# Stacking the query latent's 64-row remainder into one 128-row operand in a two-layer encoder trunk

## The chip, the cores and the metric

The kernel runs on one core of a Trainium2 chip. The metric is the device time of one execution in microseconds; three runs of the kernel before gave 1157.86 to 1158.56 us, median 1158.54 us.

## The reference

Two layers work on 256 rows of width 2048, all in float32: a gated spatial mixer (layer 0) and a latent attention (layer 1). Each is wrapped in RMS norms and shift, scale and gate that come from a condition vector. The change touches only the query path of layer 1:

```python
cq, ckv, k_rope, z = jnp.split(h @ w_in, [o1, o2, o3], axis=-1)       # o1 = 448
q = (rms_norm(cq, q_norm_g) @ w_uq).reshape(B, S, MLA_HEADS, QK_NOPE_DIM + QK_ROPE_DIM)   # 16 heads, 128 + 64
kv = (rms_norm(ckv, kv_norm_g) @ w_ukv).reshape(B, S, MLA_HEADS, QK_NOPE_DIM + V_HEAD_DIM)
q_nope, q_rope = q[..., :QK_NOPE_DIM], q[..., QK_NOPE_DIM:]
...
q_rope = apply_rope(q_rope, cos[:, None, :], sin[:, None, :])
o = chunk_causal_attention(q_nope, q_rope, k_nope, k_rope, v)
y = o.reshape(B, S, MLA_WIDTH) * jax.nn.silu(z)
return y @ w_out
```

The query's latent is 448 wide, so its product with `w_uq` contracts over 448 = 3 x 128 + 64.

## The kernel before, in words

Every large product is taken in three float32r products that stand for one float32 product. Each operand is split into a high part (a rounding cast on ScalarE) and a low part (what is left, a subtraction on VectorE); TensorE adds up high x high, high x low and low x high in PSUM. `mm` (line 184, its matmul on line 185) issues each of them.

Weights come through the class `Stream`. `weights` (line 92) makes an item: a load on SyncE's queue into one of six raw buffers, and a stage that splits it into `h` and `l` (lines 71 and 72), each out of seven buffers. `get` hands the next split item to a product and lets the stages run some items ahead. The order of loads and stages is the order in which items are listed; the engines take their instructions in the order in which the program is written (the schedule is manual), and each waits only for what it reads or for a buffer to come free.

In layer 1 the latents are computed first (chunks `pm_0`, `pm_1`), normalised per block of 128 rows in `norm_latent` (line 1014, ScalarE writes `qn` and `kvn`), then turned in `turn_latent` (line 1033) so that the latent's width lies on partitions: four transposes on TensorE for two chunks, a scaled copy on ScalarE for the high part, a subtraction on VectorE for the low part. Chunk 3 of the query latent is only 64 wide and fills 64 partitions (`ws`). The per-column gains come from `rows_b`, a tile filled by small loads on GpSimd's queue at the start (lines 200 to 207) and turned by TensorE in `turn_rows`.

Then come eight pairs of heads. `q_unit` (line 1116) makes the queries of four heads and runs four times, for `q4` = 0 to 3; `kv_unit`, `scores`, `turn_p`, `weigh` and `turn_o` run once for each pair, with products of other weights (`fill`) between them. One `q_unit` has

- `qr`: the rope part, for two row blocks, each a group of products summed into one half of a PSUM bank (64 columns of each of four heads, 256 columns),
- `rope` (line 1002), four VectorE operations for each block that read that bank and write `qr` to SBUF,
- `qn`: the part without rope, two banks of two heads, each head a group of products with 256 columns, copied out and split by ScalarE (`qH`, line 190) and VectorE (`qL`, line 191),
- later, after the `k` products of `kv_unit`, the transposes `qrT`.

That is six groups in one `q_unit` and 24 in all. A group has four chunks of the latent with three products each:

```python
for k in range(4):
    (h, l), (xh, xl) = ws[k], xs[k]
    mm(o, h[:, cs], xh, k == 0, False)
    mm(o, h[:, cs], xl, False, False)
    mm(o, l[:, cs], xh, False, k == 3)
```

For `k` = 3 the operands have 64 rows. The product banks (`acc_bank`, pool `pm`) are four. In the second, third and fourth `q_unit` two of them hold a half-done fill product, and the program makes the first product of the second `qn` bank wait for the last `rope` operation that reads the `qr` bank (line 1009 for block 1).

Of the kernel before, what the change touches and what calls it, by code (L numbers as in the profile page):

```python
# [26 lines left out]
KVR = 512  # L27
NEG = -1e30
# chunks of adaLN's rows: (first, number, the first projection's visit before which they come)
STEPS = ((0, 2, 0), (2, 2, 24), (4, 2, 45), (6, 2, 78), (8, 4, 115), (12, 4, 162))  # L30
# how far the splitting of weights runs ahead of their products, and where other work lies between them
# [19 lines left out]
# from layer 0 to layer 1: T, F, H, L turn, modulate and split block b's quarter q; g, b are products of block 0 and  # L51
# of block 1, s splits weights, c and e are what is left of layer 0
PLAN = "e1 e1 e1 e1 T00 T01 s1 F00 F01 H00 L00 H01 e1 e1 L01 T02 T03 g1 c1 F02 H02 c1 g1 g1 L02 s1 c1 c1 g1 c1 F03 c1 g1 H03 g1 L03 T11 s1 T10 F11 F10 H10 L10 g1 s1 b1 H11 b1 L11 T12 F12 H12 L12 s1 T13 b1 F13 H13 b1 b1 b1 L13 b1"
# buffers on chip
# [5 lines left out]
class Stream:  # L60
    """Weights on their way to TensorE: each item is loaded, then split into the two float32r parts, some steps
    before the products that take it. Other work that keeps step with the loads lies between the items."""
# [29 lines left out]
    def weights(self, name, src, rows=P, slot=None):  # L92
        """src: gk * rows rows, gn columns"""
        gk, gn = src.shape[0] // rows, src.shape[1]
        box = self.raw_item(name, gk, gn, [(lambda r: r[0:rows], src.rearrange("(k p) n -> p k n", p=rows))])

        def stage():
            raw = box["raw"][0:rows]
            if slot:
                h = [slot(f"{name}h_{j}", (P, gn), F32R) for j in range(gk)]  # L100
                l = [slot(f"{name}l_{j}", (P, gn), F32R) for j in range(gk)]
                for j in range(gk):
                    self.split(raw[:, j, :], h[j], l[j])
                self.ready.append((h, l))
                return
            h = self.wp.tile([P, gk, gn], F32R, tag="wh", name=name + "h", bufs=SPLIT_BUFS)
            l = self.wp.tile([P, gk, gn], F32R, tag="wl", name=name + "l", bufs=SPLIT_BUFS)
            self.split(raw, h[0:rows], l[0:rows])
            self.ready.append((h, l))

        self.stages.append((len(self.loads), True, stage))
# [23 lines left out]
def spread(main, extra):  # L135
    """the items of extra evenly between those of main"""
    if not main:
        return
    done = 0
    for i, m in enumerate(main):  # L140
        m()
        want = -(-len(extra) * (i + 1) // len(main))
        while done < want:
            extra[done]()
            done += 1
# [3 lines left out]
def tile_trunk(  # L149
# [56 lines left out]
    nc.gpsimd.dma_start(out=rows_b[35:36, 0:QR - 384], in_=mla_q_norm_g[:, 384:QR])  # L206
# [63 lines left out]
    def ada_items(name, src, width, state):  # L270
        """src(k0, nk): the columns of nk row chunks, [P, nk, width] or with a pair of column ranges between"""
        nk = 1024 // width
        todo = []
        for k in range(KD):
            def add(k=k):
                if k % nk == 0:
                    state["box"] = ST.raw_item(
                        f"{name}_{k}", nk, width,
                        [(lambda r, v=v: (r if v is None else r.rearrange("p k (t n) -> p k t n", t=2)[:, :, v, :]), a)
                         for v, a in src(k, nk)])  # L280

                def stage(box=state["box"]):
                    if k == 0:
                        state["acc"] = sp.tile([P, 1024], F32, tag="acc", name=f"acc_{name}", bufs=2)[:, 0:width]
                    acc, raw, w = state["acc"], box["raw"][:, k % nk, :], sc[:, k:k + 1]
                    if k == 0:
                        nc.vector.tensor_scalar_mul(acc, raw, w)
                    else:
                        nc.vector.scalar_tensor_tensor(acc, raw, w, acc, op0=ALU.mult, op1=ALU.add)  # L289

                ST.hook(stage)
            todo.append(add)
        return todo
# [11 lines left out]
    def ada_put(l, k, n, ps_shift, ps_scale):  # L305
        """shift and scale of chunks k .. k + n from the sums"""
# [15 lines left out]
    def ada_range(l, k0, nk):  # L322
        """shift and scale of nk column chunks"""
        st = {}
        n = nk * P
        return ada_items(
            f"ada_{l}_{k0}",
            lambda k, m: [(t, ada_rows(l, k, m, t * D + k0 * P, n)) for t in range(2)],
            2 * n, st) + [lambda: ST.hook(ada_cols(l, k0, nk, st))]

    def ada_gate(l):
        """gate times post_g, as columns"""
# [20 lines left out]
    def spread_gate(l):  # L353
        """the gate as rows on all partitions, by way of a row in DRAM"""
# [36 lines left out]
    def chain(*fns):  # L391
        """the first now, each of the others one step later"""
        fns[0]()
        if len(fns) > 1:
            deferred.append(lambda: chain(*fns[1:]))

    def chunk_tasks(name, ks, lhs, evac, per=2):
        """one 512-column chunk of a product: tasks for both blocks, one pair for each granule of the weights"""
# [26 lines left out]
    # normalised, modulated rows turned for TensorE  # L425
# [24 lines left out]
    def hT_steps(k0, nk):  # L450
        """the same in steps that lie apart, each engine's part on its own"""
# [36 lines left out]
    # the first projection's cells: row chunks of h taken as their shift and scale come  # L488
# [42 lines left out]
    # the first two chunks' shift and scale, on the way to the first product: TensorE takes a part of the rows itself  # L531
# [18 lines left out]
    def first_split():  # L550
        """the first weights' parts row chunk by row chunk, each as the products need it"""
# [70 lines left out]
    def uq_items(q4):  # L622
        c0, cw = q4 * 4 * QK, 4 * QK
        return [lambda k=k: ST.weights(f"uq_{q4}_{k}", mla_w_uq[k * P:min(k * P + P, QR), c0:c0 + cw],
                                       min(P, QR - k * P)) for k in range(4)]
# [8 lines left out]
    def fills(z, a, b):  # L634
        """what lies between the steps of a pair of heads, and what is left for after the last"""
# [332 lines left out]
    def go(n):  # L968
        """the next n granules' products of block 0"""
# [44 lines left out]
    def norm_latent(b):  # L1014
# [4 lines left out]
        nc.scalar.mul(t[:, 0:QR], l0[:, 0:QR], rq)  # L1019
        qn.append(t)  # L1020
# [12 lines left out]
    def turn_latent(src, width, gcol, name, k, H, L):  # L1033
# [5 lines left out]
        ws = [(i, min(P, width - (k + i) * P)) for i in range(2)]  # L1039

        def turn():
            for i, w in ws:
                for b in range(NB):
                    nc.tensor.transpose(out=ps[0:w, i * 256 + b * P:i * 256 + (b + 1) * P],
                                        in_=src[b][:, (k + i) * P:(k + i) * P + w], identity=ident)

        def high():
            for i, w in ws:
                nc.scalar.mul(h[0:w, i, :], ps[0:w, i * 256:(i + 1) * 256], gcol(k + i)[0:w, :])

        def low():
            for i, w in ws:
                nc.vector.scalar_tensor_tensor(l[0:w, i, :], ps[0:w, i * 256:(i + 1) * 256], gcol(k + i)[0:w, :],
                                               h[0:w, i, :].bitcast(F32), op0=ALU.mult, op1=ALU.subtract)
# [3 lines left out]
    # shared rope keys, once above zeros and once below, for the heads of a pair  # L1058
# [31 lines left out]
    turn_latent(qn, QR, qg_col, "cq", 0, cqH, cqL)  # L1090
    run(t[1:2])
    turn_latent(qn, QR, qg_col, "cq", 2, cqH, cqL)
    run(t[2:3])
    turn_latent(kvn, KVR, kvg_col, "ck", 0, ckH, ckL)
    run(t[3:4])
    turn_latent(kvn, KVR, kvg_col, "ck", 2, ckH, ckL)
# [19 lines left out]
    def q_unit(q4):  # L1116
        gs = take(4)
        ws = [(h[0:min(P, QR - k * P), 0, :], l[0:min(P, QR - k * P), 0, :]) for k, (h, l) in enumerate(gs)]
        xs = []
        for k in range(4):  # L1120
            w = min(P, QR - k * P)
            xs.append((cqH[k // 2][0:w, k % 2, :], cqL[k // 2][0:w, k % 2, :]))
        ps = acc_bank(f"qr_{q4}")
        for b in range(NB):
            bs = slice(b * P, (b + 1) * P)
            o = ps[:, b * 256:(b + 1) * 256]
            for k in range(4):
                (h, l), (xh, xl) = ws[k], xs[k]
                hr = h.rearrange("p (h r) -> p h r", r=QK)[:, :, NOPE:QK]
                lr = l.rearrange("p (h r) -> p h r", r=QK)[:, :, NOPE:QK]  # L1130
                mm(o, xh[:, bs], hr, k == 0, False)
                mm(o, xh[:, bs], lr, False, False)
                mm(o, xl[:, bs], hr, False, k == 3)
# [5 lines left out]
        for p in range(2):  # L1139
            ps = acc_bank(f"qn_{q4}_{p}")  # L1140
            for i in range(2):
                o = ps[:, i * 256:(i + 1) * 256]
                cs = slice((2 * p + i) * QK, (2 * p + i) * QK + NOPE)
                for k in range(4):
                    (h, l), (xh, xl) = ws[k], xs[k]
                    mm(o, h[:, cs], xh, k == 0, False)
                    mm(o, h[:, cs], xl, False, False)
                    mm(o, l[:, cs], xh, False, k == 3)
# [247 lines left out]
```

## Time and profile before

| | |
|---|---|
| median of three runs | 1158.54 us (1157.86 to 1158.56) |
| profiled execution | span 1157.2 us from the first to the last instruction; the page gives no other time for it |
| TensorE busy | 98% of the span, 5705 matmuls |
| VectorE, ScalarE, GpSimd busy | 77%, 49%, 2% |
| DMA | 303.57 MB, mean 262 GB/s |
| mean granted TensorE clock | 0.998 |

The page gives shares over the whole span; the attention stage that the change touches lies from about 897 to 1075 us. A timeline row has the start, the duration, the engine, the line, the operation and, in brackets, how long the engine stood idle before it and for whom. A matmul's duration includes its passage through the array, so matmuls overlap: their pace is the distance between two starts.

### The profile page before, as it was taken

The page shows a single profiled execution, that of the slowest core. Times are in us where ns is not written, and L with a number is a line of the kernel's source. Part 1 is how long each engine was busy: PE and PEld are TensorE (multiplying, and loading weights), DVE is VectorE, ACT ScalarE, POOL GpSimd, SP SyncE. Part 2 cuts the span into 40 slices and gives each one's busy share as a digit, 9 for nine tenths or more (in the row PEclk, how much of TensorE's full clock was granted, in tenths as well). Part 3 has the DMA queues.
Part 4 walks back from the last instruction along what each step waited for, and adds up shares of the span by engine and source line. Part 5 has one row for each costly group of instructions (what it writes and reads, how often), then busy time and mean ns, then how long its engine had stood idle before and what let it go on. Part 6 is the DMA issues. An engine that isn't in the chain of part 4 may idle for free.

```text
span 1157.2 us, 15835 instructions
## 1 busy us (share of the span) xinstructions
PE 1132.1 (98%) x5705; PEld 958.9 (83%) x5705; DVE 892.2 (77%) x1187; ACT 566.8 (49%) x811; POOL 20.4 (2%) x46
## 2 busy tenths in 40 slices
PE   5999999999999999999999999999999999999997
PEld 5788878888888888888888888888888989999885
DVE  4889898978987887888787878668777557558655
ACT  3764334354546655545443444456554445445541
POOL 1000000000000000000001000000000000000000
PEclk9999999999999999999999999999999999999999
DMA  9999898978887886888689999954988245245672
GB/s 317 328 322 321 273 364 290 370 254 277 298 293 232 288 272 230 280 272 284 226 315 371 356 318 373 360 175 148 342 310 293 61 136 166 68 145 183 226 271 86
DMA packets 157855, 303.57 MB, mean 262 GB/s; under 512 B 11961, under 2 KB 28960, under 8 KB 157776
## 3 DMA queue, kind: packets, MB, share of 16 engines
q1 hardware_dynamic: 155808, 297.05, 75.0%
q0 software_dynamic: 1936, 5.49, 1.7%
q8 instruction: 45, 0.74, 0.3%
q14 instruction: 34, 0.28, 0.1%
q10 hardware_dynamic: 32, 0.01, 0.0%
HBM read 300.39 MB, written 2.11 MB: 261 GB/s over the span
## 4 chain that ended last, share of the span: by engine, by line
PE 87%; DMA 4%; DVE 4%; ACT 2%; issue 2%; SPq 0%; DVEq 0%; ACTq 0%
PE pi L185 23%; PE piz L185 15%; PE po L185 15%; PE pm L185 11%; PE pp L185 8%; PE qn L185 3%; DMA wi<-in_sgu_w_in_dram 2%; PE k L185 2%; PE v L185 2%; PE s L185 2%; PE o L185 1%; PE qr L185 1%; PE pada L301 1%; PE mix L185 1%; DMA first<-in_ada_w_dram 1%
## 5 line engine op out<-in xcount | busy, mean ns | idle before, releaser
L289 DVE SCALAR_TENSOR_TENSOR acc_ada<-ada,sc,acc_ada 128x1024 f32<-128x1024 f32 (+1 forms) x135 | 148.6, 1100 | 1.1 <-DMA ada<-in_ada_w_dram 0.2
L289 DVE SCALAR_TENSOR_TENSOR acc_gate<-gate,sc,acc_gate 128x1024 f32<-128x1024 f32 x60 | 76.6, 1277 | 0.6 <-DMA gate<-in_ada_w_dram 0.6
L669 DVE TENSOR_TENSOR part<-pi,part 128x512 f32<-128x512 f32 x92 | 59.6, 682 | 4.8 <-PE pi L185 4.7
L71 ACT CAST wi_6h<-wi 128x1024 fp32r<-128x1024 f32 x24 | 25.1, 1051 | 42.3 <-DMA wi<-in_sgu_w_in_dram 35.8
L71 ACT CAST wi_8h<-wi 128x1024 fp32r<-128x1024 f32 x24 | 25.2, 1050 | 27.8 <-DMA wi<-in_sgu_w_in_dram 18.2
L71 ACT CAST wi_4h<-wi 128x1024 fp32r<-128x1024 f32 x24 | 25.2, 1050 | 27.5 <-DMA wi<-in_sgu_w_in_dram 24.3
L72 DVE TENSOR_TENSOR wi_10l<-wi,wi_10h 128x1024 fp32r<-128x1024 f32 x24 | 29.3, 1219 | 6.8 <-ACT wi_10h L71 6.8
L72 DVE TENSOR_TENSOR wi_12l<-wi,wi_12h 128x1024 fp32r<-128x1024 f32 x24 | 29.2, 1217 | 5.2 <-ACT wi_12h L71 5.2
L72 DVE TENSOR_TENSOR wi_6l<-wi,wi_6h 128x1024 fp32r<-128x1024 f32 x24 | 29.2, 1218 | 4.9 <-ACT wi_6h L71 4.9
L72 DVE TENSOR_TENSOR wi_14l<-wi,wi_14h 128x1024 fp32r<-128x1024 f32 x24 | 29.3, 1220 | 4.6 <-ACT wi_14h L71 4.6
L72 DVE TENSOR_TENSOR wi_8l<-wi,wi_8h 128x1024 fp32r<-128x1024 f32 x24 | 29.3, 1219 | 2.8 <-ACT wi_8h L71 2.5
L72 DVE TENSOR_TENSOR wi_4l<-wi,wi_4h 128x1024 fp32r<-128x1024 f32 x24 | 29.2, 1218 | 2.8 <-ACT wi_4h L71 2.7
L71 ACT CAST wi_2h<-wi 128x1024 fp32r<-128x1024 f32 x24 | 25.2, 1051 | 11.9 <-DMA wi<-in_sgu_w_in_dram 11.4
L72 DVE TENSOR_TENSOR wi_0l<-wi,wi_0h 128x1024 fp32r<-128x1024 f32 x23 | 28.1, 1221 | 3.3 <-ACT wi_0h L71 3.3
L1240 ACT ACTIVATE sm<-sm,nm 128x128 f32<-128x128 f32 (+1 forms) x32 | 14.3, 449 | 32.4 <-DVE nm L1238 32.4
L72 DVE TENSOR_TENSOR wi_2l<-wi,wi_2h 128x1024 fp32r<-128x1024 f32 x24 | 29.3, 1219 | 1.2 <-ACT wi_2h L71 1.1
L71 ACT CAST wi_0h<-wi 128x1024 fp32r<-128x1024 f32 x23 | 24.0, 1051 | 12.5 <-DMA wi<-in_sgu_w_in_dram 12.5
L71 ACT CAST wi_10h<-wi 128x1024 fp32r<-128x1024 f32 x24 | 25.1, 1045 | 10.0 <-DMA wi<-in_sgu_w_in_dram 7.7
L71 ACT CAST wi_14h<-wi 128x1024 fp32r<-128x1024 f32 x24 | 25.1, 1045 | 7.0 <-DMA wi<-in_sgu_w_in_dram 4.6
L71 ACT CAST wi_12h<-wi 128x1024 fp32r<-128x1024 f32 x24 | 25.1, 1048 | 5.0 <-PE pi L185 3.3
L185 PE MATMUL pi<-wi_4h,hH 128*128 128x512 f32 x64 | 25.3, 395 | 1.4 <-DVE part L669 1.4
L763 DVE SCALAR_TENSOR_TENSOR part<-mix,cols,part 128x256 f32<-128x256 f32 x32 | 13.3, 477 | 16.4 <-PE mix L185 16.4
(682 smaller groups left out, 3827.3 us busy)
## 6 DMA issues: line engine op xcount, KB each, us to landing
wi<-in_sgu_w_in_dram SPq DMA_DIRECT2D x191, 512.0 KB, 5.4
ada<-in_ada_w_dram SPq DMA_DIRECT2D x240, 256.0 KB, 5.2
gate<-in_ada_w_dram SPq DMA_DIRECT2D x64, 512.0 KB, 5.4
wo<-in_sgu_w_out_dram SPq DMA_DIRECT2D x64, 512.0 KB, 5.9
wm<-in_mla_w_in_dram SPq DMA_DIRECT2D x48, 512.0 KB, 5.6
wp<-in_mla_w_out_dram SPq DMA_DIRECT2D x32, 512.0 KB, 5.2
ukv<-in_mla_w_ukv_dram SPq DMA_DIRECT2D x16, 512.0 KB, 4.7
uq<-in_mla_w_uq_dram SPq DMA_DIRECT2D x12, 384.0 KB, 3.3
```

Of the source, the lines that this page charges most:

```text
L71: self.nc.scalar.copy(out=h, in_=src)
L72: self.nc.vector.tensor_tensor(out=l, in0=src, in1=h.bitcast(F32), op=ALU.subtract)
L185: nc.tensor.matmul(o, lhsT=l, rhs=r, start=start, stop=stop)
L289: nc.vector.scalar_tensor_tensor(acc, raw, w, acc, op0=ALU.mult, op1=ALU.add)
L301: nc.tensor.matmul(ps[:, j:j + 1], lhsT=state["acc"][:, j * P:(j + 1) * P], rhs=ones[:, 0:1], start=True, stop=True)
L669: nc.vector.tensor_tensor(out=part[n, b], in0=ps, in1=part[n, b], op=ALU.add)
L763: nc.vector.scalar_tensor_tensor(u[:, cs], ps[:, cs], bs_col(2 * j + i), u[:, cs], op0=ALU.add, op1=ALU.mult)
L1240: nc.scalar.activation(sm[:, i, :], sm[:, i, :], AF.Exp, bias=nm[:, i:i + 1], scale=scale, accum_out=su[:, i:i + 1])
```

## The change

The 64-wide chunk 3 of the query latent is laid out twice: `norm_latent` writes its 64 columns a second time next to themselves, so that the transposes put the same values on partitions 0 to 63 and 64 to 127; the high part is taken on all 128 partitions, and on partitions 64 to 127 it is then overwritten by the low part. The operand is now high over low. The weights of the chunk are loaded twice, once for each half; their high part is taken on all 128 partitions, their low part on partitions 0 to 63, with zeros below. High over low times the doubled high weights gives high x high plus low x high; high over low times (low weights over zeros) gives high x low. A group has 11 products, all with 128 rows.

```diff
+HK = QR - 3 * P
...
-    def weights(self, name, src, rows=P, slot=None):
+    def weights(self, name, src, slot=None):
+        rows = min(P, src.shape[0])
         gk, gn = src.shape[0] // rows, src.shape[1]
-        box = self.raw_item(name, gk, gn, [(lambda r: r[0:rows], src.rearrange("(k p) n -> p k n", p=rows))])
+        box = self.raw_item(name, gk, gn, [(lambda r, p=p: r[p:p + rows], src.rearrange("(k p) n -> p k n", p=rows))
+                                           for p in range(0, P, rows)])
...
-            self.split(raw, h[0:rows], l[0:rows])
+            if rows < P:
+                self.nc.gpsimd.memset(l[rows:P].bitcast(F32), 0.0)
+            self.nc.scalar.copy(out=h, in_=raw)
+            self.nc.vector.tensor_tensor(out=l[0:rows], in0=raw[0:rows], in1=h[0:rows].bitcast(F32), op=ALU.subtract)
...
-    nc.gpsimd.dma_start(out=rows_b[35:36, 0:QR - 384], in_=mla_q_norm_g[:, 384:QR])
+    for i in range(2):
+        nc.gpsimd.dma_start(out=rows_b[35:36, i * HK:(i + 1) * HK], in_=mla_q_norm_g[:, 384:QR])
...
         nc.scalar.mul(t[:, 0:QR], l0[:, 0:QR], rq)
+        nc.scalar.mul(t[:, QR:512], l0[:, 384:QR], rq)
...
-    def turn_latent(src, width, gcol, name, k, H, L):
+    def turn_latent(src, gcol, name, k, H, L, stacked=None):
...
         def low():
-            for i, w in ws:
-                nc.vector.scalar_tensor_tensor(l[0:w, i, :], ps[0:w, i * 256:(i + 1) * 256], gcol(k + i)[0:w, :],
-                                               h[0:w, i, :].bitcast(F32), op0=ALU.mult, op1=ALU.subtract)
+            for i in range(2):
+                r = slice(HK if k + i == stacked else 0, P)
+                o = h if k + i == stacked else l
+                nc.vector.scalar_tensor_tensor(o[r, i, :], ps[r, i * 256:(i + 1) * 256], gcol(k + i)[r, :],
+                                               h[r, i, :].bitcast(F32), op0=ALU.mult, op1=ALU.subtract)
...
     def q_unit(q4):
         gs = take(4)
...
+        parts = []
         for k in range(4):
-            w = min(P, QR - k * P)
-            xs.append((cqH[k // 2][0:w, k % 2, :], cqL[k // 2][0:w, k % 2, :]))
+            h, l = (g[:, 0, :] for g in gs[k])
+            xh, xl = cqH[k // 2][:, k % 2, :], cqL[k // 2][:, k % 2, :]
+            parts += [(xh, h), (xl, h), (xh, l)] if k < 3 else [(xh, h), (xh, l)]
+        last = len(parts) - 1
...
+            for i, (xv, w) in enumerate(parts):
+                mm(o, xv[:, bs], w.rearrange("p (h r) -> p h r", r=QK)[:, :, NOPE:QK], i == 0, i == last)
...
+                for j, (xv, w) in enumerate(parts):
+                    mm(o, w[:, cs], xv, j == 0, j == last)
```

On TensorE, in the second `q_unit`, the first group of `qr` (block 0) stood in the program like this (`uq_3h` and `uq_3l` are the parts of the 64-row weights, `cqh` and `cql` those of the latent; a size is that of the output):

```order
L185 MATMUL qr_8242<-uq_0h,cqh_7421 128x256 [waits DVE_49]
L185 MATMUL qr_8242<-uq_0l,cqh_7421 128x256
L185 MATMUL qr_8242<-uq_0h,cql_7422 128x256
L185 MATMUL qr_8242<-uq_1h,cqh_7421 128x256 [waits Activation_49]
L185 MATMUL qr_8242<-uq_1l,cqh_7421 128x256
L185 MATMUL qr_8242<-uq_1h,cql_7422 128x256
L185 MATMUL qr_8242<-uq_2h,cqh_7451 128x256 [waits Activation_49]
L185 MATMUL qr_8242<-uq_2l,cqh_7451 128x256
L185 MATMUL qr_8242<-uq_2h,cql_7452 128x256
L185 MATMUL qr_8242<-uq_3h,cqh_7451 128x256 [waits Activation_49]
L185 MATMUL qr_8242<-uq_3l,cqh_7451 128x256 [waits DVE_49]
L185 MATMUL qr_8242<-uq_3h,cql_7452 128x256
```

With the change the same group is this:

```order
L191 MATMUL qr_8243<-uq_0h,cqh_7424 128x256 [waits DVE_49]
L191 MATMUL qr_8243<-uq_0h,cql_7425 128x256
L191 MATMUL qr_8243<-uq_0l,cqh_7424 128x256
L191 MATMUL qr_8243<-uq_1h,cqh_7424 128x256 [waits Activation_49]
L191 MATMUL qr_8243<-uq_1h,cql_7425 128x256
L191 MATMUL qr_8243<-uq_1l,cqh_7424 128x256
L191 MATMUL qr_8243<-uq_2h,cqh_7454 128x256 [waits Activation_49]
L191 MATMUL qr_8243<-uq_2h,cql_7455 128x256
L191 MATMUL qr_8243<-uq_2l,cqh_7454 128x256
L191 MATMUL qr_8243<-uq_3h,cqh_7454 128x256 [waits Activation_49]
L191 MATMUL qr_8243<-uq_3l,cqh_7454 128x256 [waits DVE_49,Pool_49]
```

The product of `cql` with `uq_3h` is gone, the second and third product of a chunk have changed places in `qr`, and the product with `uq_3l` waits for GpSimd too.

On GpSimd's queue, the end of the program before (`krd` holds the shared rope keys, `gline` and `pg` spread the last gate):

```order
L1026 MEMSET krd_7214 128x256 [waits PE_49]
L1026 MEMSET krd_7265 128x256 [waits DMASW4_49,DVE_49,PE_49]
L360 DMA gline_10239<-grow_10237 16x128 [waits Activation_49]
L363 DMA pg_0_10241<-gline_10239 128x512 [waits DMASW1_49,DVE_49,DMASW2_49,PE_49,Pool_49]
L363 DMA pg_1_10243<-gline_10239 128x512 [waits PE_49]
```

With the change:

```order
L1034 MEMSET krd_7216 128x256 [waits PE_49]
L1034 MEMSET krd_7268 128x256 [waits DMASW5_49,DVE_49,PE_49]
L112 MEMSET uq_3l 64x768 [waits DVE_49,PE_49,Pool_49]
L112 MEMSET uq_3l 64x768 [waits DVE_49,PE_49] x3
L367 DMA gline_10226<-grow_10224 16x128 [waits Activation_49]
L370 DMA pg_0_10228<-gline_10226 128x512 [waits DMASW2_49,DMASW3_49,DVE_49,PE_49]
```

Four memsets, one for each `q_unit`, stand between the rope keys and the last gate; each waits until the buffer of the low weights is free.

## Rows read from the trace of the kernel before

**Rows 1.** The page's busy times of the engines over the whole span.

```profile
PE 1132.1 (98%) x5705; PEld 958.9 (83%) x5705; DVE 892.2 (77%) x1187; ACT 566.8 (49%) x811; POOL 20.4 (2%) x46
```

**Rows 2.** The chain that ended last, from 920 to 967 us: start, us, what.

```profile
920.58 2.88 PE v L185 x24
...
935.43 3.43 PE qr L185 x24
938.86 7.25 PE qn L185 x48
946.11 3.07 PE k L185 x24
...
964.48 2.87 PE k L185 x24
```

**Rows 3.** Stage of the second `q_unit` and pair: busy us, clock, DMA share, GB/s.

```profile
935.40:981.60 46.20, 45.83 (x327) 41.99 (x326) 30.59 (x67) 22.52 (x43) 0.00 (x0) 1.00 0.46 145
```

**Rows 4.** TensorE's timeline, the end of one `qn` group and the next.

```profile
941.54 0.28 PE L185 MATMUL qn<-cql,uq_2h 128*128 128x256 f32 x1
941.66 0.28 PE L185 MATMUL qn<-cqh,uq_2l 128*128 128x256 f32 x1
941.87 0.38 PE L185 MATMUL qn<-cqh,uq_3h 64*128 64x256 f32 x1
942.09 0.28 PE L185 MATMUL qn<-cql,uq_3h 64*128 64x256 f32 x1
942.21 0.28 PE L185 MATMUL qn<-cqh,uq_3l 64*128 64x256 f32 x1
942.42 0.38 PE L185 MATMUL qn<-cqh,uq_0h 128*128 128x256 f32 x1
942.64 0.28 PE L185 MATMUL qn<-cql,uq_0h 128*128 128x256 f32 x1
```

**Rows 5.** TensorE's timeline, start of the second `q_unit`.

```profile
935.19 0.36 PE L185 MATMUL qr<-uq_0h,cqh 128*128 128x256 f32 x1
935.39 0.28 PE L185 MATMUL qr<-uq_0l,cqh 128*128 128x256 f32 x1
```

**Rows 6.** VectorE's timeline, second `q_unit`.

```profile
935.21 0.95 DVE L72 TENSOR_TENSOR uq_3l<-uq,uq_3h 64x768 fp32r<-64x768 f32 x1 [1.94 <-ACT uq_3h L71]
...
937.91 1.22 DVE L72 TENSOR_TENSOR ukv_2l<-ukv,ukv_2h 128x1024 fp32r<-128x1024 f32 x1
939.04 0.28 DVE L1007 TENSOR_TENSOR qrt_0t<-qr,tab 128x128 f32<-128x128 f32 x1
...
940.63 0.41 DVE L1009 TENSOR_TENSOR qr<-qr,tab 128x256 f32<-128x256 f32 x1
```

**Rows 7.** The same, third `q_unit`, where the rope waits for TensorE.

```profile
985.06 0.29 DVE L1007 TENSOR_TENSOR qrt_0t<-qr,tab 128x128 f32<-128x128 f32 x1 [1.54 <-PE qr L185]
...
986.66 0.41 DVE L1009 TENSOR_TENSOR qr<-qr,tab 128x256 f32<-128x256 f32 x1
```

**Rows 8.** TensorE's waits from 885 to 1050 us: us in total, times, longest.

```profile
PE o L185 <- DVE pL L191: 0.7, 2, 0.4
```

**Rows 9.** GpSimd's timeline: a small load and a memset at the start.

```profile
4.12 0.51 POOL L206 DMA_DIRECT2D rows_b<-in_mla_q_norm_g_dram  x1
...
5.11 0.44 POOL L216 MEMSET maskb<- 128x384 f32 x1
```

**Rows 10.** TensorE's timeline, where `rows_b` is first read.

```profile
20.70 0.45 PE L230 MATMUL pcol<-ident,rows_b 128*128 128x128 f32 x1
```

**Rows 11.** The chunk's split: the tile `uq_3h`, its casts and the first product of `qr` with it.

```profile
L185 PE MATMUL qr<-uq_3h,cqh x8: 383/384/387, 898.9 to 1030.0; 64*128 64x256 f32 x8
...
L71 ACT CAST uq_3h<-uq x4: 817/839/840, 889.5 to 1017.8; 64x768 fp32r<-64x768 f32 x4
```

**Rows 12.** ScalarE's timeline, `norm_latent` of block 0.

```profile
832.25 0.33 ACT L1022 ACTIVATE kvn<-lat,rk_0i 128x64 f32<-128x64 f32 x1
```

**Rows 13.** Loads of the 64-row weights, 880 to 1050 us: count, KB each, us to landing.

```profile
uq<-in_mla_w_uq_dram SPq DMA_DIRECT2D x4, 192.0 KB, 3.5
```

**Rows 14.** The tile `wsn`: GpSimd's memsets in layer 0.

```profile
L717 POOL MEMSET wsn<- x4: 301/304/307, 196.3 to 521.3; 64x256 f32 x4
```

More of the change, by code (lines that the diff above doesn't have):

```diff
@@ L90, in raw_item @@
         return box
-    def weights(self, name, src, rows=P, slot=None):
+    def weights(self, name, src, slot=None):
+        rows = min(P, src.shape[0])
         gk, gn = src.shape[0] // rows, src.shape[1]
-        box = self.raw_item(name, gk, gn, [(lambda r: r[0:rows], src.rearrange("(k p) n -> p k n", p=rows))])
+        box = self.raw_item(name, gk, gn, [(lambda r, p=p: r[p:p + rows], src.rearrange("(k p) n -> p k n", p=rows))
+                                           for p in range(0, P, rows)])
         def stage():
-            raw = box["raw"][0:rows]
+            raw = box["raw"]
             if slot:
@@ L623, in uq_items @@
         c0, cw = q4 * 4 * QK, 4 * QK
-        return [lambda k=k: ST.weights(f"uq_{q4}_{k}", mla_w_uq[k * P:min(k * P + P, QR), c0:c0 + cw],
-                                       min(P, QR - k * P)) for k in range(4)]
+        return [lambda k=k: ST.weights(f"uq_{q4}_{k}", mla_w_uq[k * P:min(k * P + P, QR), c0:c0 + cw])
+                for k in range(4)]
     def ukv_items(hp):
@@ L1038, in turn_latent @@
         L.append(l)
-        ws = [(i, min(P, width - (k + i) * P)) for i in range(2)]
         def turn():
-            for i, w in ws:
+            for i in range(2):
                 for b in range(NB):
-                    nc.tensor.transpose(out=ps[0:w, i * 256 + b * P:i * 256 + (b + 1) * P],
-                                        in_=src[b][:, (k + i) * P:(k + i) * P + w], identity=ident)
+                    nc.tensor.transpose(out=ps[:, i * 256 + b * P:i * 256 + (b + 1) * P],
+                                        in_=src[b][:, (k + i) * P:(k + i + 1) * P], identity=ident)
         def high():
-            for i, w in ws:
-                nc.scalar.mul(h[0:w, i, :], ps[0:w, i * 256:(i + 1) * 256], gcol(k + i)[0:w, :])
+            for i in range(2):
+                nc.scalar.mul(h[:, i, :], ps[:, i * 256:(i + 1) * 256], gcol(k + i))
         def low():
-            for i, w in ws:
-                nc.vector.scalar_tensor_tensor(l[0:w, i, :], ps[0:w, i * 256:(i + 1) * 256], gcol(k + i)[0:w, :],
-                                               h[0:w, i, :].bitcast(F32), op0=ALU.mult, op1=ALU.subtract)
+            for i in range(2):
+                r = slice(HK if k + i == stacked else 0, P)
+                o = h if k + i == stacked else l
+                nc.vector.scalar_tensor_tensor(o[r, i, :], ps[r, i * 256:(i + 1) * 256], gcol(k + i)[r, :],
+                                               h[r, i, :].bitcast(F32), op0=ALU.mult, op1=ALU.subtract)
         chain(turn, high, low)
@@ L1089, in tile_trunk @@
     run(t[:1])
-    turn_latent(qn, QR, qg_col, "cq", 0, cqH, cqL)
+    turn_latent(qn, qg_col, "cq", 0, cqH, cqL)
     run(t[1:2])
-    turn_latent(qn, QR, qg_col, "cq", 2, cqH, cqL)
+    turn_latent(qn, qg_col, "cq", 2, cqH, cqL, stacked=3)
     run(t[2:3])
-    turn_latent(kvn, KVR, kvg_col, "ck", 0, ckH, ckL)
+    turn_latent(kvn, kvg_col, "ck", 0, ckH, ckL)
     run(t[3:4])
-    turn_latent(kvn, KVR, kvg_col, "ck", 2, ckH, ckL)
+    turn_latent(kvn, kvg_col, "ck", 2, ckH, ckL)
     run(t[4:5])
@@ L1117, in q_unit @@
         gs = take(4)
-        ws = [(h[0:min(P, QR - k * P), 0, :], l[0:min(P, QR - k * P), 0, :]) for k, (h, l) in enumerate(gs)]
-        xs = []
+        parts = []
         for k in range(4):
-            w = min(P, QR - k * P)
-            xs.append((cqH[k // 2][0:w, k % 2, :], cqL[k // 2][0:w, k % 2, :]))
+            h, l = (g[:, 0, :] for g in gs[k])
+            xh, xl = cqH[k // 2][:, k % 2, :], cqL[k // 2][:, k % 2, :]
+            parts += [(xh, h), (xl, h), (xh, l)] if k < 3 else [(xh, h), (xh, l)]
+        last = len(parts) - 1
         ps = acc_bank(f"qr_{q4}")
@@ L1126, in q_unit @@
             o = ps[:, b * 256:(b + 1) * 256]
[L1127 to L1133, printed above, removed]
+            for i, (xv, w) in enumerate(parts):
+                mm(o, xv[:, bs], w.rearrange("p (h r) -> p h r", r=QK)[:, :, NOPE:QK], i == 0, i == last)
         qr = slot(f"qr_{q4}", (P, NB, 4, ROPE))
@@ L1143, in q_unit @@
                 cs = slice((2 * p + i) * QK, (2 * p + i) * QK + NOPE)
[L1144 to L1148, printed above, removed]
+                for j, (xv, w) in enumerate(parts):
+                    mm(o, w[:, cs], xv, j == 0, j == last)
             h = slot(f"qH_{q4}_{p}", (P, 2, 256), F32R)
```

## The prediction

> **What bounds the kernel now.** The first view is the page's table of busy times: TensorE is busy for 98% of the span, VectorE for 77%, ScalarE for 49% [rows 1]. A share over the whole span says little about one stage, so the second view is the busy time in the stretch of the second `q_unit` and its pair: TensorE 45.83 of 46.20 us, VectorE 30.59, ScalarE 22.52, DMA share 0.46, granted clock 1.00 [rows 3]. The third is the chain that ended last: here it runs from one TensorE group to the next, `qr`, `qn`, `k` [rows 2]. The fourth is the list of TensorE's waits from 885 to 1050 us: one line, 0.7 us in two waits, in the `o` products [rows 8]. So TensorE's own stream sets the pace of the attention, and time taken off it comes off the end, until something that TensorE waits for is late.
>
> The fifth view is the timeline of that stream, and the reader is to look at distances between starts. The `k` products have the same 256 columns and 128 rows throughout: 24 in 2.87 us, 0.1196 us each [rows 2], in the `k` of 964.48, which follows no 64-row product. A group of `qn` has 12 products, and 48 take 7.25 us, so a group takes 1.8125 us, 0.38 us more than 12 x 0.1196 = 1.435. The rows show where it lies: starts are 0.12 us apart, but at the step from 128 to 64 rows they are 0.21 and 0.22 apart, and again 0.21 and 0.22 at the step back [rows 4]. Each step costs some 0.19 us. The `k` that follows `qn` pays for the last step back: 3.07 instead of 2.87 [rows 2].
>
> **The change part by part.**
>
> *Products.* A group loses one product of twelve, and all eleven left have 128 rows. Six groups in each of four `q_unit`s make 24. If the pace is that of `k`, a group takes 11 x 0.1196 = 1.316 us in place of 1.8125, 0.497 less, and 24 groups 11.9 us less. Only 24 x 0.1196 = 2.9 us of it are the products; 9.0 us are the steps between row counts. Check on one unit: `qr`, `qn` and the `k` behind them take 3.43 + 7.25 + 3.07 = 13.75 us [rows 2]; 66 + 24 products at 0.1196 take 10.76; 2.99 less, four times 12.0. I take 11.9.
>
> Here a rule speaks against the larger part. The Trainium skill, page "TensorE: Matmul & The Clock Gate", says under "Why this matters for your kernels" that a product over 32 rows takes the same time as one over 128, and under "Part 2" that a weight load's time goes by its columns, not its rows. By that alone the gain would be the 24 products, 2.9 us. The rows bear it out inside a run of 64-row products (0.12 apart, as with 128 rows) but not at the step from one row count to the other, and the sum goes by the rows. The same notes, page "TensorEngine Tiling (Array Packing)", "Key Properties", say that changing the tiling mode drains the engine, which names a cause that fits the gaps.
>
> *The wait for the `qr` bank.* The second `qn` bank's first product waits for the last rope operation that reads the `qr` bank. A faster TensorE comes to it earlier. In the second `q_unit` `qr` starts at 935.19 and steps to its second product at 935.39 [rows 5]; 21 more steps of 0.1196 put the first `qn` product at 937.90, and 22 more the second bank at 940.53. The rope there starts at 939.04 not because of TensorE but because VectorE is held by weight splits (the last began at 937.91), which hang on the scores before and not on `qr`; its last read ends at 940.63 + 0.41 = 941.04 [rows 6]. So TensorE waits 0.5 us, with some 0.1 for the signal 0.6. In the third unit the rope does wait for `qr` [rows 7], so it moves with it: it ends its reads 986.66 + 0.41 - 985.06 = 2.0 us after it starts, and it would start some 0.2 us after the first `qn` product does (a product lasts 0.28 and the next starts 0.12 after it) [rows 4]. The bank is then free at 2.2 and wanted at 22 x 0.1196 = 2.6: 0.4 to spare. I take the same for the fourth; in the first the banks are free otherwise. Given back: 0.6 us.
>
> *The wait for GpSimd.* The product with `uq_3l` now waits for a memset of 64 x 768. No such memset is in the trace; 128 x 384 took 0.44 us [rows 9], so I estimate 0.9. It may start when the buffer is free, which is when TensorE has ended a product of earlier weights. In the first unit the cast of `uq_3h` waits for that buffer's pair and starts at 889.5; TensorE reads the chunk at 898.9 [rows 11]: 9.4 us of room. In the second the buffer's last readers are the `v` products that end at 920.58 + 2.88 = 923.46 [rows 2], some 13 us before the read; the third and fourth are built alike. On GpSimd nothing but the last gate stands behind the memsets. Cost 0; if the room were gone, 0.9 a unit.
>
> *Splits.* The cast takes 128 partitions in place of 64 with the same 768 columns, and the tile shows 0.84 us for 64 [rows 11]; the first three chunks are casts of 128 x 768 already. VectorE's subtraction stays at 64 partitions: in the second unit it ends at 935.21 + 0.95 = 936.16 [rows 6], and TensorE comes to it at 935.39 + 9 x 0.1196 = 936.47, in time by 0.3. That is the narrowest cover here; were it gone, TensorE would wait as long as the split is late.
>
> *Loads.* Four loads of 192 KB more on SyncE's queue, 3.5 us to landing each [rows 13], in a stretch with a DMA share of 0.46 [rows 3] and with weights that land several items ahead. Cost 0.
>
> *Latents.* Two more ScalarE operations of 128 x 64 at 0.33 us [rows 12], two chunk steps ahead of their transposes, whose number stays. At the start one more small load of 0.51 us on GpSimd's queue [rows 9]; its tile, `rows_b`, is read at 20.7 us [rows 10], 15 us later. Cost 0 for both.
>
> **The sum.** 11.9 - 0.6 = 11.3 us less. The profiled execution goes from 1157.2 to 1145.9 us of span; the median of the runs is 1.3 us above its span, which I leave as it is: 1158.5 - 11.3 = 1147.2 us.
>
> **The rivals.**
>
> *The rope sets the pace in more units.* The 0.4 us to spare in the third and fourth unit rest on the rope moving up with `qr`. If VectorE held it there as it does in the second unit, TensorE would wait another 0.5 us in each: 1148.2. For it: VectorE is the second busiest engine here [rows 3]. Against it: in the third unit it stood idle for 1.54 us before the rope [rows 7].
>
> *The gaps stay, only products go.* If the gaps belonged to the chunk's place in the group or to another tensor, and not to the row count, they would stay, and the gain is 24 x 0.1196 = 2.9 us: 1155.6. This is what the clock page's rule gives. Against it: a group of `k` has no such gap at its fourth chunk, nor where it takes up the next tensor, and the gaps lie on both sides of the 64-row products [rows 2, 4]. That the change does not do what it says is excluded by the program's order, with 11 products in a group, and by the diff, which takes the operands whole.
>
> *The memset is late: slower.* GpSimd's memset writes the buffer while VectorE subtracts, and TensorE waits for it. It costs nothing up to 9.4 us, and from there on a microsecond for each one, four times; the kernel is slower than before once it lasts longer than 9.4 + 11.3 / 4 = 12.2 us. At 14 us it would be 1147.2 + 4 x 4.6 = 1165.6. A rule makes this a rival: the Trainium skill, "GPSIMD Engine Reference", "Key points", says that GpSimd shares its SBUF interfaces with VectorE and contends with instructions that have two SBUF inputs, as the split's subtraction has. Against it: four memsets of 64 x 256 in layer 0, under a VectorE that is busy for 77% of the span [rows 1], lasted 301 to 307 ns [rows 14], a third of my estimate for three times the columns; the memset would have to be 13 times as long.
>
> **How the numbers follow.** The forecast has 0.81, the rope in more units 0.11, the gaps that stay 0.06, the late memset 0.02. The predicted time is the forecast's, 1147.2. Its unknowns: no wait for the rope at all (0.6 less), the waits of the first rival (1.0 more), some 0.7 either way between single runs, and a last half microsecond for small costs taken as zero. That makes 1145.8 to 1149.4, which holds the first two cases, less some for sizes that I have wrong; the other two are the left out. A measurement of this kernel can tell about 0.2%, 2.3 us, from no change. Faster by more: the first two cases and most of the third, 0.95; within it: 0.03; slower: 0.02.
>
> **What would show it.** In the profile after, 22 `qr` and 44 `qn` products in the chain at some 2.6 and 5.3 us a unit, a `k` behind `qn` of 2.87, and no distance between starts over 0.13 us inside a group; a matmul count 24 lower; one wait of TensorE at `qn` for the rope, about half a microsecond, in the second unit; memsets of about 0.9 us that end well ahead of the product with `uq_3l`. It is wrong if gaps of 0.2 us still stand at the fourth chunk, if TensorE's list of waits has lines that add up to over 2 us, or if time is lost outside 897 to 1045 us.

## The result and the profile after

The changed kernel takes 1147.7 us (median of four runs, 1147.31 to 1148.33), the kernel before 1158.55 us beside it: a ratio of 0.9904 with a 95% interval from 0.9892 to 0.9916, so 9.7 to 12.5 us less. The forecast was 1147.2 us in a range of 1145.8 to 1149.4. The span of the profiled execution fell from 1157.2 to 1145.7 us.

The first line of the profile after, the busy times over the whole span, says little, as [rows 1] did: TensorE is at 98% again, with 24 matmuls fewer.

```profile
PE 1120.1 (98%) x5681; PEld 953.2 (83%) x5681; DVE 892.8 (78%) x1187; ACT 567.6 (50%) x813; POOL 23.9 (2%) x51
```

The chain that ended last shows where the time went (start, us, what). These are the first, third and fourth `q_unit` of the changed kernel, to be read against [rows 2]:

```profile
897.74 2.63 PE qr L191 x22
900.38 5.28 PE qn L191 x44
905.66 2.88 PE k L191 x24
...
976.27 2.62 PE qr L191 x22
978.90 5.28 PE qn L191 x44
984.18 2.88 PE k L191 x24
...
1018.88 2.63 PE qr L191 x22
1021.50 5.28 PE qn L191 x44
1026.78 2.88 PE k L191 x24
```

A unit with its `k` takes 2.63 + 5.28 + 2.88 = 10.79 us, where it took 13.75: 2.96 less. The first `qr` starts at 897.74, 0.1 us from its old 897.86, and the `k` of the last pair at 1044.36 in place of 1055.62, so 11.1 of the 11.5 us between the spans were gained in the stage that was changed. The rest, 0.12 ahead of it and 0.24 behind it, lies where both kernels have the same products; in the runs below the first `qr` starts anywhere between 896.9 and 898.5, so no more is read into it.

The timeline of TensorE in the second `q_unit` shows the step at the fourth chunk gone, and the wait that took a part of the gain:

```profile
933.14 0.28 PE L191 MATMUL qr<-uq_2l,cqh 128*128 128x256 f32 x1
933.26 0.28 PE L191 MATMUL qr<-uq_3h,cqh 128*128 128x256 f32 x1
933.38 0.28 PE L191 MATMUL qr<-uq_3l,cqh 128*128 128x256 f32 x1
933.50 0.28 PE L191 MATMUL qr<-uq_0h,cqh 128*128 128x256 f32 x1
...
937.34 0.28 PE L191 MATMUL qn<-cqh,uq_3l 128*128 128x256 f32 x1
938.11 0.36 PE L191 MATMUL qn<-cqh,uq_0h 128*128 128x256 f32 x1 [0.49 <-DVE qr L1016]
938.31 0.28 PE L191 MATMUL qn<-cql,uq_0h 128*128 128x256 f32 x1
```

Into the fourth chunk and out of it the starts are 0.12 us apart, where [rows 4] has two of 0.21 and 0.22 at each step. From 937.34 to 938.11 they are 0.77 apart: the second `qn` bank waits for the rope. VectorE's timeline shows why, as [rows 6] did before; its rope starts late and has its last read of the bank at the end of the second row:

```profile
935.97 0.28 DVE L1014 TENSOR_TENSOR qrt_0t<-qr,tab 128x128 f32<-128x128 f32 x1
...
937.55 0.41 DVE L1016 TENSOR_TENSOR qr<-qr,tab 128x256 f32<-128x256 f32 x1
```

TensorE's waits from 870 to 1050 us (us in total, times, longest) have one line more than [rows 8]:

```profile
PE o L191 <- DVE pL L197: 0.7, 2, 0.4
PE qn L191 <- DVE qr L1016: 0.5, 1, 0.5
```

GpSimd's memset lasts 0.74 us and starts, in the first unit, as soon as the buffer is free:

```profile
889.70 0.74 POOL L112 MEMSET uq_3l<- 64x768 f32 x1 [95.48 <-PE pm L191]
```

### The profile page after: what moved, and what is told of

The parts are those of the page before. It is cut to its first block, busy times and chain, and to the rows that moved or that the text cites. A ratio compares the mean times of both kernels' runs of the same rounds, so it can differ in the third digit from the quotient of the medians.

```text
span 1145.7 us, 15806 instructions
## 1 busy us (share of the span) xinstructions
PE 1120.1 (98%) x5681; PEld 953.2 (83%) x5681; DVE 892.8 (78%) x1187; ACT 567.6 (50%) x813; POOL 23.9 (2%) x51
## 4 chain that ended last, share of the span: by engine, by line
PE 86%; DMA 5%; DVE 4%; ACT 2%; issue 2%; SPq 0%; DVEq 0%; ACTq 0%
PE pi L191 23%; PE piz L191 15%; PE po L191 15%; PE pm L191 10%; PE pp L191 8%; DMA wi<-in_sgu_w_in_dram 2%; PE k L191 2%; PE v L191 2%; PE s L191 2%; PE qn L191 2%; DMA ada<-in_ada_w_dram 1%; PE o L191 1%; PE pada L308 1%; PE mix L191 1%; DMA first<-in_ada_w_dram 1%
## 5 line engine op out<-in xcount | busy, mean ns | idle before, releaser
L113 ACT CAST wi_0h<-wi 128x1024 fp32r<-128x1024 f32 x23 | 24.0, 1051 | 12.5 <-DMA wi<-in_sgu_w_in_dram 12.5
```

Of the source, the lines that this page charges most:

```text
L113: self.nc.scalar.copy(out=h, in_=raw)
```

## The experiments

The theory: a step between 64 and 128 rows costs TensorE 0.19 us, 48 of them 9.0 us, the 24 products 2.9 us; what the change adds is hidden, but for the wait for the rope. The rivals: the gaps belong to the chunk's place or to the end of a group and not to the row count; the additions cost something; the memset and VectorE get in each other's way; the wait at `qn` comes from something else.

**Twelve products of 128 rows.** The stacking is undone and the row count kept:

```diff
-        nc.scalar.mul(t[:, QR:512], l0[:, 384:QR], rq)
+        nc.gpsimd.memset(t[:, QR:512], 0.0)
...
-    turn_latent(qn, qg_col, "cq", 2, cqH, cqL, stacked=3)
+    turn_latent(qn, qg_col, "cq", 2, cqH, cqL)
...
-            parts += [(xh, h), (xl, h), (xh, l)] if k < 3 else [(xh, h), (xh, l)]
+            parts += [(xh, h), (xl, h), (xh, l)]
```

> The changed kernel without the stacking: the 64-wide chunk is padded to 128 rows with zeros in the latent, the weights are loaded doubled as in the change, and a group has 12 products again, all of 128 rows. Theory (the steps between row counts cost 0.19 us each, 48 of them): the 9.0 us of the steps go, the 2.9 us of the products do not; 1158.5 - 9.0 = 1149.5 us, plus some 0.1 us of waiting for the rope in the second query unit. A group is 12 x 0.12 = 1.44 us with no distance between starts over 0.13. Rival (the gain is the product count, the gaps belong to the fourth chunk or its tensors): 1158.5 us, with gaps at the fourth chunk.

Measured: 1150.07 us, ratio 0.9928 (0.9910 to 0.9946). The chain, first unit:

```profile
897.98 2.87 PE qr L191 x24
900.85 5.76 PE qn L191 x48
906.61 2.88 PE k L191 x24
```

These are 11.51 us in place of 13.75, so 2.24 us less in a unit and 9.0 in four, with as many products as before. The changed kernel's 10.79 lie another 0.72 lower, 2.9 us in four units. Three quarters of the gain have nothing to do with there being fewer products. The second unit has another 0.24 us at the start of its second `qn` bank, where the rope is late in this kernel too; 0.1 was expected.

**Half the steps.** In the kernel before, every second group takes its chunks in the reverse order (shown for `qn`; `qr` has the same by block):

```diff
-                for k in range(4):
+                ks = range(4) if i == 0 else range(3, -1, -1)
+                for k in ks:
                     (h, l), (xh, xl) = ws[k], xs[k]
-                    mm(o, h[:, cs], xh, k == 0, False)
+                    mm(o, h[:, cs], xh, k == ks[0], False)
                     mm(o, h[:, cs], xl, False, False)
-                    mm(o, l[:, cs], xh, False, k == 3)
+                    mm(o, l[:, cs], xh, False, k == ks[-1])
```

> The kernel before, with the chunks of every second group in the reverse order (3, 2, 1, 0), so that the 64-row products of two groups follow each other: the same 288 products, 24 steps between row counts in place of 48. Theory: 24 x 0.19 = 4.5 us less, 1154.0 us; the gaps stand only where the row count changes, and none lies between the two groups' 64-row products. Rival (a gap at the begin and end of a group, or at the change of the weights' tile): the gaps stay as many, 1158.5 us.

Measured: 1153.69 us, ratio 0.9961 (0.9947 to 0.9975). TensorE's timeline where two groups of `qr` meet:

```profile
935.28 0.28 PE L185 MATMUL qr<-uq_2h,cql 128*128 128x256 f32 x1
935.49 0.38 PE L185 MATMUL qr<-uq_3h,cqh 64*128 64x256 f32 x1
935.71 0.28 PE L185 MATMUL qr<-uq_3l,cqh 64*128 64x256 f32 x1
935.83 0.28 PE L185 MATMUL qr<-uq_3h,cql 64*128 64x256 f32 x1
935.95 0.28 PE L185 MATMUL qr<-uq_3h,cqh 64*128 64x256 f32 x1
936.07 0.28 PE L185 MATMUL qr<-uq_3l,cqh 64*128 64x256 f32 x1
936.19 0.28 PE L185 MATMUL qr<-uq_3h,cql 64*128 64x256 f32 x1
936.39 0.38 PE L185 MATMUL qr<-uq_2h,cqh 128*128 128x256 f32 x1
936.62 0.28 PE L185 MATMUL qr<-uq_2l,cqh 128*128 128x256 f32 x1
```

One group ends at 935.83 and the next begins at 935.95, 0.12 us later: a group's end costs nothing. The gaps of 0.2 stand only where the sizes in the row change from 128 rows to 64 and back. A unit with its `k` took 3.24 + 6.49 + 2.88 = 12.61 us, 1.14 less than before, 4.6 in four against 4.5 expected.

**Three times the steps.** The other way: in every group of the kernel before, the three 64-row products stand after the third, the sixth and the eighth of the nine 128-row products, so that none has another beside it:

```diff
+SCAT = (0, 1, 2, 9, 3, 4, 5, 10, 6, 7, 11, 8)
...
+                for j, i in enumerate(SCAT):
+                    mm(o, pr[i][0], pr[i][1], j == 0, j == 11)
```

> The kernel before, with the three 64-row products of each group set apart between the 128-row products (after the third, the sixth and the eleventh product but one), the same 288 products: six steps between row counts in a group in place of two. Theory (0.19 us a step, whatever the place): 24 x 4 = 96 steps more, 18.2 us, 1176.7 us; a group of 12 x 0.12 + 6 x 0.19 = 2.57 us. Rival (only the first entry into the fourth chunk's tile and the end of the group cost something): 1158.5 us.

Measured: 1177.23 us in a single run, 18.6 more than the kernel before beside it (1158.62); 18.2 were expected for 96 steps more. The chain, first unit:

```profile
897.70 5.15 PE qr L186 x24
902.86 10.32 PE qn L186 x48
913.18 2.88 PE k L186 x24
```

A group of `qn` takes 10.32 / 4 = 2.58 us, which is 12 x 0.1196 and six steps of 0.19. The price of a step is the same with one, two and six of them in a group; the rivals about the chunk's place have fallen.

**Only what stands around the products.** Loads, casts, memsets and doubled latents as in the change, with the old twelve products, the fourth chunk's on 64 rows:

```diff
-    turn_latent(qn, qg_col, "cq", 2, cqH, cqL, stacked=3)
+    turn_latent(qn, qg_col, "cq", 2, cqH, cqL)
...
+            if k == 3:
+                h, l, xh, xl = h[0:HK], l[0:HK], xh[0:HK], xl[0:HK]
-            parts += [(xh, h), (xl, h), (xh, l)] if k < 3 else [(xh, h), (xh, l)]
+            parts += [(xh, h), (xl, h), (xh, l)]
```

> All that the change adds, without its products: doubled loads, casts on 128 partitions, memsets, doubled latent columns and gains; the products are the old 12 with 64 rows in the fourth chunk (the low part below is unused). Theory (all of that is hidden): 1158.5 us, the gaps of 0.2 us at the fourth chunk as before. Rival (loads, casts or memsets cost time that the change's gain had to pay for): 0.5 to 1 us more than 1158.5.

Measured: 1158.58 us, ratio 0.9996 (0.9987 to 1.0006). The additions cost nothing that can be told, at most 0.7 us more. That holds at the old pace, at which TensorE comes to its operands later than in the changed kernel; for the new pace the list of TensorE's waits above stands. The memset is not on TensorE's path in this kernel, since nothing reads the zeros; that is the next run's part.

**The memset sixteen times.**

```diff
-                self.nc.gpsimd.memset(l[rows:P].bitcast(F32), 0.0)
+                for _ in range(16):
+                    self.nc.gpsimd.memset(l[rows:P].bitcast(F32), 0.0)
```

> The changed kernel with each of the four memsets done 16 times over. One takes 0.74 us in the changed kernel's trace, 16 take 11.8. Theory (each has its cover, from the buffer's release to the product that reads it: 9.1 us in the first query unit, 13.4 and more in the others): TensorE waits 2.7 us for GpSimd in the first unit and not in the others; 1147.7 + 2.7 = 1150.4 us, a memset still at 0.74 us, VectorE's splits at 0.95 and 1.23. Rival (GpSimd and VectorE get in each other's way): memsets well over 0.74 us or splits well over 1.23, TensorE waiting in all four units, 5 us or more.

Measured: 1152.89 us in a single run, 5.2 us over the changed kernel, not 2.7. GpSimd's timeline and TensorE's waits, first the sixteen memsets of the first unit:

```profile
889.41 12.62 POOL L113 MEMSET uq_3l<- 64x768 f32 x16 [95.47 <-PE pm L192]
```

```profile
PE qr L192 <- POOL uq_3l L113: 3.4, 1, 3.4
PE o L192 <- DVE pL L198: 0.7, 2, 0.4
PE qn L192 <- DVE qr L1017: 0.6, 1, 0.6
PE qr L192 <- DVE uq_3l L115: 0.2, 1, 0.2
```

The wait is in the first unit alone, as expected, and 3.4 us long, since a memset comes every 0.79 us and not every 0.74. A memset still takes 0.74 us and the split of the same tile 0.945 (0.946 in the changed kernel), so GpSimd and VectorE do not slow each other here, and that rival has fallen. The 0.2 us at `qr` for VectorE stand in the second unit, where the split of `uq_3l` ends too late by that much. Most of the rest is TensorE's clock. The stretches after the wait (us, PE busy, PEld, DVE, ACT, POOL, clock, DMA share, GB/s):

```profile
898.70:902.00 3.30, 0.00 (x0) 0.00 (x0) 1.23 (x1) 0.32 (x1) 3.07 (x5) 1.00 0.21 32
902.00:904.00 2.00, 1.92 (x13) 1.92 (x14) 0.00 (x0) 0.00 (x0) 0.03 (x1) 0.83 0.37 144
904.00:906.00 2.00, 2.00 (x12) 2.00 (x11) 1.88 (x7) 0.00 (x0) 0.00 (x0) 0.50 0.03 8
906.00:908.00 2.00, 2.00 (x16) 2.00 (x16) 0.52 (x2) 0.06 (x1) 0.00 (x0) 0.82 0.00 0
908.00:910.00 2.00, 2.00 (x19) 2.00 (x18) 0.69 (x1) 0.53 (x1) 0.00 (x0) 1.00 0.00 0
```

TensorE stood still for 3.4 us, worked again from 902.1, and only then fell to a granted clock of 0.50, the 1.2 GHz level, until some time between 906 and 908. The `qn` behind the wait took 6.49 us in place of 5.28. From its first `qr` product to its first `k` product the unit took 13.1 us (897.29 to 910.38) in place of 7.9 (897.58 to 905.49), 5.2 more. The wait is 3.6 of it (two starts 3.71 apart in place of 0.12), so it cost some 1.6 us more than its own length.

**The rope bank copied, in all four units.** ScalarE copies the bank of `qr` to on-chip memory, and the rope reads the copy:

```diff
-        qv = ps.rearrange("p (b h r) -> p b h r", b=NB, r=ROPE)
+        qc = slot(f"qc_{q4}")
+        nc.scalar.copy(out=qc, in_=ps)
+        qv = qc.rearrange("p (b h r) -> p b h r", b=NB, r=ROPE)
```

> The changed kernel, where ScalarE first copies the rope part's PSUM bank to on-chip memory and the rope reads the copy. Theory (the 0.5 us that TensorE waits in the second query unit is for the bank that the late rope still reads): the wait is gone, the second unit's bank is free some 0.6 us after its last rope product, 1147.7 - 0.5 = 1147.2 us, read from TensorE's waits and the chain rather than from the time, which cannot tell half a microsecond. Rival (VectorE's backlog of splits itself holds TensorE there): the wait moves to another product of the same unit and the time stays at 1147.7.

Measured: 1149.86 us, ratio 0.9922 (0.9908 to 0.9935): no faster than the changed kernel, although the wait at `qn` is gone. The chain has 2.62 and 5.28 us for the second unit, and TensorE's waits in the whole span have no line for `qn`, but 1.3 us in three waits at `o`. The timeline of TensorE in the first pair, and the granted clock behind it:

```profile
923.69 0.33 PE L191 MATMUL o<-vH,pL 128*128 128x128 f32 x1 [0.52 <-DVE pL L197]
...
925.28 0.33 PE L191 MATMUL o<-vH,pL 128*128 128x128 f32 x1 [0.37 <-DVE pL L197]
```

```profile
925.00:926.00 1.00, 0.72 (x6) 0.72 (x7) 1.00 (x2) 0.00 (x0) 0.00 (x0) 1.00 0.94 336
926.00:927.00 1.00, 1.00 (x8) 1.00 (x7) 0.85 (x5) 0.00 (x0) 0.00 (x0) 0.58 0.71 268
...
932.00:933.00 1.00, 1.00 (x4) 0.72 (x4) 0.48 (x3) 0.39 (x1) 0.00 (x0) 0.51 0.05 20
933.00:934.00 1.00, 1.00 (x6) 0.83 (x5) 0.00 (x0) 1.00 (x5) 0.00 (x0) 1.00 0.00 0
```

Two waits of 0.52 and 0.37 us stand within two microseconds in the first pair, where the changed kernel has one; behind them the clock is at 0.50 until 933. The 24 score products right behind the waits, those of the second pair, took 5.22 us there and 2.82 in the changed kernel (926.19 to 929.01). The new wait goes back to ScalarE: the chain that ended last runs from the load of its activation table, ahead of the first softmax, to the product that waited 0.52 us. That load ran at 913.50 in the changed kernel and at 914.61 here, although the first `qr` starts 0.8 us earlier here (896.93), and here it waited 1.96 us for VectorE, which it did not do before. First the row of the changed kernel, then that of this one:

```profile
913.50 1.28 ACT L1245 ACT_TABLE_LOAD   x1
```

```profile
914.61 1.28 ACT L1247 ACT_TABLE_LOAD   x1 [1.96 <-DVE nm L1245]
```

**The copy in the second unit alone**, which leaves that table load as it was:

```diff
-        qv = ps.rearrange("p (b h r) -> p b h r", b=NB, r=ROPE)
+        qc = slot(f"qc_{q4}") if q4 == 1 else None
+        if q4 == 1:
+            nc.scalar.copy(out=qc, in_=ps)
+        qv = (qc if q4 == 1 else ps).rearrange("p (b h r) -> p b h r", b=NB, r=ROPE)
```

> The changed kernel with ScalarE's copy of the rope bank in the second query unit alone, which leaves the wait of the activation table load after the first pair's scores where the changed kernel has it (in the run with four copies that load came 1.1 us later and TensorE waited twice in the first pair's o products before its clock fell). Theory (the copy removes the 0.5 us wait; the fall of the clock came from the waits in the first pair): no wait at qn, waits at o of 0.7 us as in the changed kernel, clock 1.00 from 897 to 1050 us, 1147.2 us, half a microsecond under the changed kernel on the same chip. Rival (the copy itself costs): the waits at o or the fall of the clock come back, 1149 to 1150 us.

**The changed kernel beside it**, on the same chip:

> The changed kernel unaltered, on the same chip and beside the run before it: 1147.7 us, one wait of 0.5 us at qn, so that half a microsecond can be looked for between the two.

Measured: 1146.22 us with the copy, ratio 0.9893 (0.9877 to 0.9910), and 1147.67 us without, ratio 0.9901 (0.9886 to 0.9915). With the copy the second unit reads like the others, TensorE's waits from 870 to 1050 us are those of the kernel before, and the granted clock is 1.00 from 897 to 1050 us:

```profile
931.59 2.63 PE qr L191 x22
934.22 5.28 PE qn L191 x44
939.50 2.88 PE k L191 x24
```

```profile
PE o L191 <- DVE pL L197: 0.7, 2, 0.4
```

The unaltered kernel has its wait of 0.5 us at `qn` again. So the wait is explained, and the copy takes it away. Whether the version is faster the intervals cannot tell, as they overlap. Of the 1.4 us between the two profiled spans (1145.6 and 1144.2), 0.6 lie ahead of the first `qr`, where the kernels are the same.

## Why the prediction was right

*Products and steps, 11.9 us.* Right in the sum and in its parts: 2.96 us a unit against 2.98 (a quarter of 11.9), of which 2.24 are the steps (the padded kernel) and 0.72 the products. By the rule that only the products count, the kernel would have stood at 1155.6 us. The padded kernel and the two kernels that move the steps show that the rule holds for a run of 64-row products and leaves out what it costs to go in and out of it. The page "TensorEngine Tiling (Array Packing)" of the Trainium skill says under "Key Properties" that changing the tiling mode drains the engine, which fits the gaps; no run here shows whether a step in rows is such a change, or what happens in the array.

*The wait for the rope, 0.6 us in the second unit alone.* Right in place, cause and size: 0.77 us between two starts in place of 0.12, so 0.65, and some 0.1 at the next start. The rope starts 3.86 us after the first `qr` product (932.11 to 935.97), 3.85 before (935.19 to 939.04): as forecast, it hangs on what stands ahead of the unit and not on `qr`. The copy took the wait away.

*The other units.* The 0.4 us to spare in the third and fourth were enough: the bank is free at 980.94 and wanted at 981.37 in the third, 1023.55 and 1023.98 in the fourth, and neither has a wait.

*The memset.* Estimated at 0.9 us from 128 x 384, measured 0.74. The cover of 9.4 us came out at 9.1 (889.70 to 898.77), and sixteen memsets end 3.4 us after TensorE wants them. The rival's price was wrong: it charges a late memset in all four units from 9.4 us on and puts the break-even with the kernel before at 12.2 us, though the prediction itself counts 13 us of cover in the other units. With 12.6 us of memsets TensorE waited in the first unit alone, and the kernel took 1152.89 us, still less than before.

*Splits, loads, latents at 0.* Right within what the run of them alone can tell. The narrowest cover, 0.3 us at the split of `uq_3l` in the second unit, came out as forecast (the split ends at 933.08, its product starts at 933.38); with the memset sixteen times it was gone, and TensorE waited 0.2 us there.

*The median.* The 0.5 us between 1147.2 and 1147.7, no more than single runs of the changed kernel differ by, can be put down to one term: the 1.3 us between the span and the median. I took the difference between one execution's span and another set's median for a constant. In the runs that list both, time less span is 1.7 to 1.9 us, for every kernel. The profiled execution before was thus at some 1159.0, above the median, and the forecast span of 1145.9 us with 1.8 added is 1147.7. That the span came within 0.2 us of its forecast is in part luck: the changed stage gave 11.1 us against 11.3, and 0.4 came from stages that the forecast leaves as they are.

## What to carry to other kernels

On an engine that is busy all the time, look at the distances between starts before counting instructions: here the leftover chunk's three products cost 0.36 us a group and going in and out of their row count another 0.38. Filling the remainder up to the full row count was worth 9 us here even with zeros and no product fewer, since its products stand between full ones; filling it with useful work gave another 2.9. The price of a step was measured for this one size of product, so for others it has to be read from their own starts. When a busy engine gets faster, look for the buffer it now comes to too early, and price that wait with the clock behind it.

## What the runs showed of the hardware

A wait of TensorE can cost more than its length. In the kernel with sixteen memsets TensorE had no work for 3.4 us, the granted clock was at 0.50 (1.2 GHz) while it was already busy again, and the loss was 5.2 us. Behind two waits of 0.52 and 0.37 us the clock was at 0.50 for some 6.8 us in the profiled execution of the four-copy kernel; four of its five runs list a mean clock of 0.995 or 0.996 and 1149.3 to 1150.4 us, the fifth 0.998 and 1147.33 us. The changed kernel's single waits of 0.4 and 0.5 us leave the clock at 1.00 from 897 to 1050 us. That the two waits made the clock fall is likely from their place, and the kernel with one copy has neither the second wait nor the fall; but no run added a wait of half a microsecond by itself, so it is not shown.
